# A sixth raw weight tile, in room taken from a work tile, the squares' buffer and the mixer's masks

## The chip, the cores and the metric

The kernel runs on one core of one Trainium2 chip. Its metric is the device time of one execution in microseconds (us). TensorE (PE) multiplies, VectorE (DVE) and ScalarE (ACT) prepare operands, GpSimd (POOL) and SyncE (SP) mostly issue transfers (DMAs).

## The reference

One layer of a decoder trunk, in float32: two feed-forward blocks around a mixer, with RMSNorm ahead of each and at the end.

```python
def rmsnorm(x, g):
    x32 = x.astype(jnp.float32)
    y = x32 * lax.rsqrt(jnp.mean(x32 * x32, axis=-1, keepdims=True) + EPS)
    return (y * g.astype(jnp.float32)).astype(x.dtype)

def swiglu(h, w_gate, w_up, w_down):
    return (jax.nn.silu(h @ w_gate) * (h @ w_up)) @ w_down
```
```text
x = x + 0.5 * SwiGLU_1(RMSNorm(x))
h = RMSNorm(x)
[attn_q|attn_k|attn_v|m_q|m_k|m_v|m_o|m_i|m_f] = h @ W_in
y_A = differential attention (4 heads, causal; weights a[0] - lam * a[1], lam from exps of two sums of lambda products)
y_B = mLSTM matrix memory (4 heads, causal conv on q/k, exp input gate, sigmoid forget gate, chunks of 128)
x = x + concat(y_A, y_B) @ W_out
x = x + 0.5 * SwiGLU_2(RMSNorm(x))
out = RMSNorm_final(x)
```

256 positions, model width 2048, feed-forward width 5632. All weights are float32 and each is read from memory once.

## The kernel before

**Products in two parts.** A float32 product is made of three single-pass products. Each weight tile `w` is split into `wh`, its rounding to the fast format (fp32r, a cast on ACT, line 132), and `wl = w - wh` (a subtraction on DVE, line 133); the activations are split the same way. PE then runs `wh*xh` (L181), `wh*xl` (L182) and `wl*xh` (L184). The parts lie in a pool of four pairs.

**Paired chunks.** Most weights go through the class `Paired`, which computes two output chunks of 512 columns (gate and up, or two neighbours) with fewer products than one by one, from sums of weight tiles. `load` (L446 and L208) fetches one raw tile, `raw`, with 256 KB of the one matrix and 512 KB of the other; a chunk has five such tiles (two or three in the down projections), fetched through POOL's queue, or SP's for the first chunks. `leading` multiplies the first slot and makes sums in place on DVE (L479); `second_sum` multiplies them and adds again, by an accumulating DMA on POOL (`raw<-raw`, L495) or on DVE (L497); `sums` adds a third weight tile `late` by accumulating DMA (`raw<-late`, L533), copies two finished banks with ACT into the work tiles `ds` and `us` (L503), and subtracts them on DVE (L537, L546). `second` and `third` follow, with unpaired weight tiles `rawp` (L219) between. A `raw` tile is free when its last split is done. Such a tile comes from the pool `wr`, of five buffers.

**Pools and order.** Tiles come from pools of fixed numbers of buffers; asking for a tile when all are in use makes the first instruction on it wait for the release of the oldest. Work tiles (pool `work`, tag `w`, eight buffers of 2 KB a partition) hold `xg`, `xsum`, `hg`, `sg`, `ds`, `us`, `part` and the mixer's small tiles, the lambda vectors `lv` among them; larger tiles come from 22 `slots`. A list scheduler fixes each engine's order when the program is built, from priorities (`tc.high_priority`, `soon`) and the buffers that are free in its own account of time. On the chip each engine runs its list strictly in order and waits on semaphores.

**Finishing a chunk of the residual.** `residual` (for the first block) and `finish2` (for the last) add half of an accumulator to `xres` on DVE (L359, L1211), then take the sum of squares of that piece for the next norm with `square_sum` (L300, ACT, with a separate instruction that reads the accumulator). The squares themselves are thrown away, into a buffer `junk`, one in all, of its own pool tag. `finish2` also multiplies by the final norm's gains (`fn`, L1213). `chunk_to_xt` transposes `xres` on PE (L314) for the next product.

**The start of the mixer.** `lv` is loaded by one POOL DMA (L768), two rows of it are multiplied on DVE (L769), reduced to `lsum` (L771), and ACT takes `lexp = exp(lsum)` (L773), which needs a table load. Masks for the causal products (`mask_qk`, `mask_kq`), a bf16 identity, a matrix of ones and an upper triangle are made on POOL at the very start of the program (L106 to L122) and kept; the mixer's small columns lie in pools `const` and `small`.

## Time and profile before

| | us |
|---|---|
| median of 3 runs | 1759.2 |
| lowest and highest | 1758.26, 1760.3 |
| profiled execution, its own time | 1759.56 |
| its span (first to last instruction) | 1757.8 |
| PE busy in the span | 1744.6 |
| DVE busy | 1617.8 |
| ACT busy | 1267.4 |
| POOL busy | 429.3 |

The clock granted to TensorE was 0.999. Times within the trace count from the start of the span. In the timeline views a row is: start, duration, engine, line, operation, tile written and tiles read, shape, how many in a row, and in brackets the engine's idle time just before with what ended it. In the groups it is busy time and mean, then idle time and its releasers. L181 is line 181 of the kernel before; the changed kernel's lines are 12 to 16 lower up to the mixer.

### The profile page before, as it was taken

What the parts mean: (1) busy time and instruction counts of PE and PEld (TensorE: products, weight loads), DVE (VectorE), ACT (ScalarE), POOL (GpSimd) and SP (SyncE); (2) the same over time, 40 slices, a digit from 0 to 9 for tenths busy, and PEclk for the clock granted to TensorE, in tenths of its full rate; (3) what the DMA queues carried; (4) which work ended last, traced back from release to release, by engine and by line L of the source; (5) the groups of instructions that cost most, each with busy time, mean ns of one, the idle gap of its engine ahead of it and who ended that gap; (6) DMA issues with size and microseconds to landing.
All of it is one profiled execution on the core that took longest, in us unless ns stands there. A gap on an engine that the chain in (4) does not pass through costs nothing.

```text
span 1757.8 us, 24486 instructions
## 1 busy us (share of the span) xinstructions
PE 1744.6 (99%) x7926; PEld 1437.7 (82%) x7926; DVE 1617.8 (92%) x2189; ACT 1267.4 (72%) x1949; POOL 429.3 (24%) x630
## 2 busy tenths in 40 slices
PE   9999999999999999999999999999999999999998
PEld 7788888888888888987888888888888878888886
DVE  7999999999999999898888999999999999999997
ACT  8666777777677768777687777776777677677765
POOL 0022332322233312012231101122332332233310
PEclk9999999999999999999999999999999999999999
DMA  9787998999799977577886667898998999799973
GB/s 365 251 254 209 259 261 265 253 292 265 218 262 258 263 252 204 185 230 221 236 238 192 209 210 211 260 265 233 258 260 268 241 268 276 232 246 256 283 254 115
DMA packets 155265, 429.72 MB, mean 244 GB/s; under 512 B 17632, under 2 KB 18944, under 8 KB 154880
## 3 DMA queue, kind: packets, MB, share of 16 engines
q0 software_dynamic: 76304, 196.66, 45.1%
q1 hardware_dynamic: 77680, 229.40, 38.0%
q10 hardware_dynamic: 1152, 2.09, 0.3%
q8 instruction: 62, 1.02, 0.2%
q14 instruction: 67, 0.55, 0.1%
HBM read 349.56 MB, written 2.10 MB: 200 GB/s over the span
## 4 chain that ended last, share of the span: by engine, by line
PE 93%; DMA 2%; DVE 2%; issue 1%; ACT 0%; POOL 0%; SPq 0%; POOLq 0%; DVEq 0%; ACTq 0%
PE acc L184 18%; PE acc L181 18%; PE acc L182 18%; PE accn L181 12%; PE accn L182 12%; PE accn L184 12%; DVE wl L133 1%; DMA raw<-in_wg_dram 1%; PE tr L373 1%; DMA raw<-in_wu_dram 1%; PE tr L314 0%; PE sc L1060 0%; DMA rawp<-in_wg_dram 0%; ACT wh L132 0%; PE num L1011 0%
## 5 line engine op out<-in xcount | busy, mean ns | idle before, releaser
L132 ACT CAST wh<-raw 128x512 fp32r<-128x512 f32 (+2 forms) x885 | 601.5, 708 | 214.5 <-PE acc L182 66.3
L133 DVE TENSOR_TENSOR wl<-raw,wh 128x512 fp32r<-128x512 f32 (+2 forms) x885 | 676.1, 793 | 58.4 <-ACT wh L132 54.5
L132 ACT CAST wh<-rawp 128x1024 fp32r<-128x1024 f32 (+3 forms) x308 | 318.2, 1035 | 109.5 <-PE acc L182 55.1
L133 DVE TENSOR_TENSOR wl<-rawp,wh 128x1024 fp32r<-128x1024 f32 (+3 forms) x308 | 367.1, 1197 | 32.0 <-ACT wh L132 29.8
L181 PE MATMUL acc<-wh,xs 128*128 128x512 f32 (+2 forms) x956 | 369.5, 387 | 0.0
L182 PE MATMUL acc<-wh,xs 128*128 128x512 f32 (+2 forms) x956 | 368.9, 386 | 0.0
L184 PE MATMUL acc<-wl,xs 128*128 128x512 f32 (+2 forms) x956 | 317.6, 387 | 0.8 <-DVE wl L133 0.7
L533 POOL DMA_DIRECT2D raw<-late x176 | 152.6, 1053 | 442.7 <-DVE wl L133 422.9
L181 PE MATMUL acc<-wh,xt 128*128 128x512 f32 (+2 forms) x564 | 218.4, 388 | 0.7 <-ACT wh L132 0.7
L182 PE MATMUL acc<-wh,xt 128*128 128x512 f32 (+2 forms) x564 | 217.3, 386 | 0.0
L181 PE MATMUL accn<-wh,xt 128*128 128x512 f32 (+1 forms) x552 | 215.3, 391 | 0.0
L182 PE MATMUL accn<-wh,xt 128*128 128x512 f32 (+1 forms) x552 | 214.7, 390 | 0.0
L479 DVE TENSOR_TENSOR raw<-raw 128x1024 f32<-128x1024 f32 x176 | 211.0, 1217 | 0.8
L184 PEld LDWEIGHTS acc<-wl,xs 128*128 128x128 f32 x956 | 178.3, 188 | 39.2 <-DVE wl L133 3.6
L181 PEld LDWEIGHTS acc<-wh,xs 128*128 128x128 f32 x956 | 179.5, 188 | 36.4 <-ACT wh L132 0.6
L182 PEld LDWEIGHTS acc<-wh,xs 128*128 128x128 f32 x956 | 179.6, 188 | 35.6
L181 PE MATMUL accn<-wh,xs 128*128 128x512 f32 (+1 forms) x408 | 162.6, 400 | 1.9 <-ACT wh L132 1.9
L182 PE MATMUL accn<-wh,xs 128*128 128x512 f32 (+1 forms) x408 | 158.0, 388 | 0.0
L184 PE MATMUL acc<-wl,xt 128*128 128x512 f32 (+2 forms) x564 | 157.6, 386 | 0.0
L495 POOL DMA_DIRECT2D raw<-raw x92 | 78.9, 899 | 322.1 <-DVE wl L133 234.7
L184 PE MATMUL accn<-wl,xt 128*128 128x512 f32 (+1 forms) x552 | 154.7, 388 | 0.0
L184 PE MATMUL accn<-wl,xs 128*128 128x512 f32 (+1 forms) x408 | 140.9, 388 | 0.0
(229 smaller groups left out, 2125.0 us busy)
## 6 DMA issues: line engine op xcount, KB each, us to landing
rawp<-in_wd_dram SPq DMA_DIRECT2D x88, 512.0 KB, 5.6
raw<-late POOLq DMA_DIRECT2D x174, 256.0 KB, 5.3
raw<-in_wu_dram POOLq DMA_DIRECT2D x80, 512.0 KB, 8.4
rawp<-in_wu_dram SPq DMA_DIRECT2D x73, 512.0 KB, 5.1
rawp<-in_wg_dram SPq DMA_DIRECT2D x69, 512.0 KB, 5.2
raw<-raw POOLq DMA_DIRECT2D x92, 256.0 KB, 4.1
raw<-in_wd_dram POOLq DMA_DIRECT2D x44, 512.0 KB, 8.6
late<-in_wg_dram SPq DMA_DIRECT2D x41, 512.0 KB, 9.2
```

The source lines that it names most:

```text
L132: return (nc.scalar.copy(hi, src), nc.vector.tensor_tensor(out=lo, in0=src, in1=hi.bitcast(F32), op=ALU.subtract))
L133: nc.vector.tensor_tensor(out=lo, in0=src, in1=hi.bitcast(F32), op=ALU.subtract))
L181: nc.tensor.matmul(acc, lh, rh, start=first, stop=False, skip_group_check=on)
L182: nc.tensor.matmul(acc, ll, rh, start=False, stop=False, skip_group_check=on)
L184: newest[:] = [nc.tensor.matmul(acc, lh, rl, start=False, stop=last, skip_group_check=on)]
L373: nc.tensor.transpose(tr[:, i, hb * P:(hb + 1) * P], hs[hb][:, k * P:(k + 1) * P], ident)
L479: nc.vector.tensor_tensor(out=raw[:, 0:2, :], in0=raw[:, 0:3:2, :], in1=raw[:, 1:2, :].to_broadcast([P, 2, n]), op=ALU.add)
L495: nc.gpsimd.dma_start(raw[:, 0, :], raw[:, 2, :], accum_op=ALU.add)
L533: nc.gpsimd.dma_start(self.raws[j][:, 0, :], lates[-1][1][:, i, :], accum_op=ALU.add)
```

## The change

`wr` grows from five raw tiles to six, `work` shrinks from eight to seven. `square_sum` writes its squares into a work tile, so that they no longer have a buffer of their own. The masks, the ones, the triangle and the bf16 identity are made at the start of the mixer, on POOL, in one large tile `masks` from the slots (the identity's copy on POOL rather than on DVE), and the mixer's small columns (`lsum`, `lexp`, `nlam`, `gatt`, `gp`, the attention's maxima and sums and so on) are cut from the same tile by `ct`.

```diff
--- before.py
+++ after.py
@@ -64,8 +64,8 @@
     const = ctx.enter_context(tc.tile_pool(name="const", bufs=1))
     big = ctx.enter_context(tc.tile_pool(name="big", bufs=1))
     slots = ctx.enter_context(tc.tile_pool(name="slots", bufs=22))
-    work = ctx.enter_context(tc.tile_pool(name="work", bufs=8))
-    wr = ctx.enter_context(tc.tile_pool(name="wr", bufs=5))
+    work = ctx.enter_context(tc.tile_pool(name="work", bufs=7))
+    wr = ctx.enter_context(tc.tile_pool(name="wr", bufs=6))
     wrp = ctx.enter_context(tc.tile_pool(name="wrp", bufs=5))
     wsp = ctx.enter_context(tc.tile_pool(name="wsp", bufs=4))
     small = ctx.enter_context(tc.tile_pool(name="small", bufs=2))
@@ -103,23 +103,8 @@
     nc.gpsimd.memset(ident, 0.0)
     nc.gpsimd.affine_select(out=ident, in_=ident, compare_op=ALU.not_equal, fill=1.0, base=0,
                             pattern=[[-1, P]], channel_multiplier=1)
-    ones = const.tile([P, P], F32, name="ones")
-    nc.gpsimd.memset(ones, 1.0)
-    upper = const.tile([P, P], F32, name="upper")
-    nc.gpsimd.affine_select(out=upper, in_=ones, compare_op=ALU.is_ge, fill=0.0, base=0,
-                            pattern=[[1, P]], channel_multiplier=-1)
     mhalf = const.tile([P, 8], F32, name="mhalf")
     nc.gpsimd.memset(mhalf, -0.5)
-    ident_b = const.tile([P, P], BF16, name="ident_b")
-    nc.vector.tensor_copy(ident_b, ident)
-    mask_qk = const.tile([P, P], BF16, name="mask_qk")
-    nc.gpsimd.memset(mask_qk, 0.0)
-    nc.gpsimd.affine_select(out=mask_qk, in_=mask_qk, compare_op=ALU.is_ge, fill=NEG, base=0,
-                            pattern=[[-1, P]], channel_multiplier=1)
-    mask_kq = const.tile([P, P], BF16, name="mask_kq")
-    nc.gpsimd.memset(mask_kq, 0.0)
-    nc.gpsimd.affine_select(out=mask_kq, in_=mask_kq, compare_op=ALU.is_ge, fill=NEG, base=0,
-                            pattern=[[1, P]], channel_multiplier=-1)
     xres = big.tile([P, NT, D], F32, name="xres")
 
     def split_gain(src, gcol, hi, lo):
@@ -296,8 +281,7 @@
         return r
 
     def square_sum(src, acc, scale=1.0):
-        j = small.tile([P, CW], BF16, tag="junk", name=nm("junk"), bufs=1)
-        nc.scalar.activation(j[:, 0:src.shape[-1]], src, AF.Square, scale=scale, accum_out=acc)
+        nc.scalar.activation(wk("junk")[:, 0:src.shape[-1]], src, AF.Square, scale=scale, accum_out=acc)
 
     def finish_norm(parts):
         tot = small.tile([P, NT], F32, tag="tot", name=nm("tot"))
@@ -764,17 +748,37 @@
     bif = const.tile([P, 8], F32, name="bif")
     with tc.issue_after(splits[-30][0].ins):
         nc.scalar.dma_start(bif, bias_if.partition_broadcast(P))
+    masks = mixt([P, 8 * P], name="masks")
+    ones, upper = masks[:, 0:P], masks[:, P:2 * P]
+    nc.gpsimd.memset(ones, 1.0)
+    nc.gpsimd.affine_select(out=upper, in_=ones, compare_op=ALU.is_ge, fill=0.0, base=0,
+                            pattern=[[1, P]], channel_multiplier=-1)
+    ident_b, mask_qk, mask_kq = (masks[:, (4 + i) * P // 2:(5 + i) * P // 2].bitcast(BF16) for i in range(3))
+    nc.gpsimd.tensor_copy(ident_b, ident)
+    for mask, sign in ((mask_qk, -1), (mask_kq, 1)):
+        nc.gpsimd.memset(mask, 0.0)
+        nc.gpsimd.affine_select(out=mask, in_=mask, compare_op=ALU.is_ge, fill=NEG, base=0,
+                                pattern=[[sign, P]], channel_multiplier=-sign)
+
+    taken = [4 * P]
+
+    def ct(shape, name):
+        o = taken[0]
+        taken[0] += math.prod(shape[1:])
+        t = masks[0:shape[0], o:taken[0]]
+        return t.rearrange("p (a b) -> p a b", a=shape[1]) if len(shape) > 2 else t
+
     lv = mixt([P, 4, P], name="lv")
     nc.gpsimd.dma_start(lv, lamv.partition_broadcast(P))
     nc.vector.tensor_tensor(out=lv[:, 0:2, :], in0=lv[:, 0:2, :], in1=lv[:, 2:4, :], op=ALU.mult)
-    lsum = const.tile([P, 2], F32, name="lsum")
+    lsum = ct([P, 2], "lsum")
     nc.vector.tensor_reduce(out=lsum, in_=lv[:, 0:2, :], axis=AX.X, op=ALU.add)
-    lexp = const.tile([P, 2], F32, name="lexp")
+    lexp = ct([P, 2], "lexp")
     nc.scalar.activation(lexp, lsum, AF.Exp)
-    nlam = const.tile([P, 1], F32, name="nlam")
+    nlam = ct([P, 1], "nlam")
     nc.vector.tensor_tensor(out=nlam, in0=lexp[:, 1:2], in1=lexp[:, 0:1], op=ALU.subtract)
     nc.vector.tensor_scalar(nlam, nlam, -LAM_INIT, None, op0=ALU.add)
-    gatt = const.tile([P, 8], F32, name="gatt")
+    gatt = ct([P, 8], "gatt")
     nc.vector.tensor_scalar(gatt, prm[:, G_ATT:G_ATT + 8], 1.0 - LAM_INIT, None, op0=ALU.mult)
 
 
@@ -826,7 +830,7 @@
 
 
     mT = [mixt([P, NH, S], name="mT") for _ in range(2)]
-    gp = const.tile([P, NT, 8], F32, name="gp")
+    gp = ct([P, NT, 8], "gp")
     heads = [0, 3, 6, 8]
 
     def finish_qk(c, accs):
@@ -855,9 +859,6 @@
     chain.finish()
     accs = []
     chain.put(units(accs, xp2, wqk[2], KD), KD // UK, functools.partial(finish_qk, 2, accs))
-
-    def ct(shape, name):
-        return const.tile(shape, F32, name=name)
 
     with tc.high_priority(offset=AHEAD + 40):
         gt = ct([P, NT, 8], "gt")
@@ -1050,8 +1051,8 @@
 
     def attend(h):
         q, k, o = qT[h // 2], kT[h // 2], 2 * (h % 2)
-        mx = small.tile([P, 4], F32, tag="amx", name=nm("amx"))
-        sm = small.tile([P, 4], F32, tag="asm", name=nm("asm"))
+        mx = ct([P, 4], "amx")
+        sm = ct([P, 4], "asm")
         e = mixt([P, 2, 3 * P], name="aexp")
         for hb in range(NT):
             n = (hb + 1) * P
@@ -1071,7 +1072,7 @@
         w = mixt([P, 3 * P], name="aw")
         for hb in range(NT):
             n = (hb + 1) * P
-            nl = small.tile([P, 1], F32, tag="nl", name=nm("nl"))
+            nl = ct([P, 1], "nl")
             vec.tensor_tensor(out=nl, in0=sm[:, 2 * hb + 1:2 * hb + 2], in1=nlam, op=ALU.mult)
             sl = slice(hb * P, hb * P + n)
             vec.tensor_scalar(w[:, sl], e[:, 1, sl], nl, None, op0=ALU.mult)
@@ -1114,7 +1115,7 @@
         nc.tensor.matmul(ps[:, 0, :], wts[h][:, 0:P], vs[0], start=True, stop=True)
         nc.tensor.matmul(ps[:, 1, :], wts[h][:, P:S], vs[0], start=True, stop=False)
         nc.tensor.matmul(ps[:, 1, :], wts[h][:, S:S + P], vs[1], start=False, stop=True)
-        ss = small.tile([P, NT], F32, tag="ssa", name=nm("ssa"))
+        ss = ct([P, NT], "ssa")
         for hb in range(NT):
             square_sum(ps[:, hb, :], ss[:, hb:hb + 1])
         ra = rsq(ss, NT, float(VD), "ra")
@@ -1166,7 +1167,7 @@
         return r3[0]
 
     fn = []
-    parts4 = [small.tile([P, 4], F32, tag=f"parts4{hb}", name=f"parts4{hb}") for hb in range(NT)]
+    parts4 = [small.tile([P, 4], F32, tag=f"parts4{hb}", name=f"parts4{hb}", bufs=1) for hb in range(NT)]
 
     def store(hb, acc):
```

The arithmetic is unchanged. The scheduler orders the instructions anew, and the order moves at these places.

POOL's queue, a gate-and-up chunk of the second block near the end (L446 and L208 load a raw tile's two parts, L495 and L533 are the accumulating DMAs; L430, L193, L479 and L517 in the changed kernel). Before, from the last accumulate of one chunk on:

```order
L533 DMA raw_15270<-late_15369 128x512
L446 DMA raw_15577<-in_wg_dram 128x512
L208 DMA raw_15577<-in_wu_dram 128x1024
L446 DMA raw_15580<-in_wg_dram 128x512
L208 DMA raw_15580<-in_wu_dram 128x1024
L446 DMA raw_15615<-in_wg_dram 128x512
L208 DMA raw_15615<-in_wu_dram 128x1024
L446 DMA raw_15618<-in_wg_dram 128x512
L208 DMA raw_15618<-in_wu_dram 128x1024
L446 DMA raw_15667<-in_wg_dram 128x512
L208 DMA raw_15667<-in_wu_dram 128x1024
L495 DMA raw_15577<-raw_15577 128x512
```

Now, the same place:

```order
L517 DMA raw_15220<-late_15319 128x512
L430 DMA raw_15530<-in_wg_dram 128x512
L193 DMA raw_15530<-in_wu_dram 128x1024
L430 DMA raw_15565<-in_wg_dram 128x512
L193 DMA raw_15565<-in_wu_dram 128x1024
L430 DMA raw_15568<-in_wg_dram 128x512
L193 DMA raw_15568<-in_wu_dram 128x1024
L430 DMA raw_15617<-in_wg_dram 128x512
L193 DMA raw_15617<-in_wu_dram 128x1024
L430 DMA raw_15933<-in_wd_dram 128x512
L193 DMA raw_15933<-in_wd_dram 128x1024
L479 DMA raw_15527<-raw_15527 128x512
```

The chunk's first pair (`raw_15527`) went out ahead of the accumulates of the chunk before, and the first pair of the following one (`in_wd`) stands at the end of this group. The other paired chunks have moved alike.

DVE's queue at the start of the mixer (L133 and L118 are the splits, L359 and L343 the residual update, `lv` the lambda vectors). Before:

```order
L133 TENSOR_TENSOR wl_6608<-late_6588,wh_6607 128x784
L133 TENSOR_TENSOR wl_6618<-raw_6482,wh_6617 128x392
L133 TENSOR_TENSOR wl_6618<-raw_6486,wh_6617 128x392
L359 SCALAR_TENSOR_TENSOR xres<-acc_6120,xres 128x512
L133 TENSOR_TENSOR xs_6514<-xg_6511,xs_6514 128x512
L133 TENSOR_TENSOR wl_6635<-rawp_6632,wh_6634 128x784
L537 TENSOR_TENSOR acc_6481<-acc_6481,us_6604 128x392
L133 TENSOR_TENSOR wl_6681<-raw_6482,wh_6680 128x784
L133 TENSOR_TENSOR xs_6386<-xsum_6382,xs_6386 128x512
L546 TENSOR_TENSOR acc_6480<-ds_6586,acc_6480 128x392
L769 TENSOR_TENSOR lv_6429<-lv_6429 128x256
```

Now:

```order
L782 TENSOR_SCALAR masks_6413<-prm 128x8
L118 TENSOR_TENSOR xs_6353<-xsum_6349,xs_6353 128x512
L118 TENSOR_TENSOR xs_6370<-xsum_6366,xs_6370 128x512
L773 TENSOR_TENSOR lv_6425<-lv_6425 128x256
L343 SCALAR_TENSOR_TENSOR xres<-acc_6104,xres 128x512
L775 TENSOR_REDUCE masks_6413<-lv_6425 128x2
L118 TENSOR_TENSOR wl_6599<-late_6579,wh_6598 128x784
L118 TENSOR_TENSOR xs_6505<-xg_6502,xs_6505 128x512
L118 TENSOR_TENSOR wl_6609<-raw_6473,wh_6608 128x392
L118 TENSOR_TENSOR wl_6609<-raw_6477,wh_6608 128x392
```

The multiply of `lv`, one residual update and the reduce to `lsum` (now a column of `masks`) have moved ahead of the split of `late` and those of the raw pair; the multiply stood ten rows behind that split before. On ACT the table load and the exponential have moved with them, ahead of two squares, `ds`, `us` and the cast of the next `rawp`.

ACT's queue near the end of the second block (L132 and L117 are the casts, L300 and L284 the squares, L503 and L487 the copies `ds` and `us`). Before:

```order
L503 COPY ds_16377<-acc_16277 128x512
L132 CAST wh_16408<-late_16379 128x1024
L300 ACTIVATE junk_16255,parts_10132<-xres 128x512
L132 CAST wh_16418<-late_16395 128x512
L132 CAST wh_16425<-raw_16278 128x512
L132 CAST wh_16425<-raw_16281 128x512
L503 COPY us_16405<-acc_16276 128x512
```

Now:

```order
L117 CAST wh_16358<-late_16329 128x1024
L284 ACTIVATE junk_16205,parts_10082<-xres 128x512
L284 ACTIVATE junk_16320,parts_10081<-xres 128x512
L284 ACTIVATE junk_16324,parts_10082<-xres 128x512
L487 COPY ds_16327<-acc_16227 128x512
L487 COPY us_16355<-acc_16226 128x512
L117 CAST wh_16368<-late_16345 128x512
L117 CAST wh_16375<-raw_16228 128x512
L117 CAST wh_16375<-raw_16231 128x512
```

Two more squares, `ds` and `us` now precede the second cast of `late`. The same pattern, smaller, stands at the ends of the first block and of the output projection.

## Prediction

> **What bounds the kernel now.** I read the page's first part, then the busy time by stretches, then PE's waits, and last the timelines of the places where the order of instructions changes. The profiled execution took 1759.56 us, its span 1757.8; 1.8 us lie around the span, and I keep them. It stands 0.4 us above the median of the runs shown, 1759.2.
>
> ```profile
> PE 1744.6 (99%) x7926; PEld 1437.7 (82%) x7926; DVE 1617.8 (92%) x2189; ACT 1267.4 (72%) x1949; POOL 429.3 (24%) x630
> ...
> 0.00:20.00 20.00, 16.80 (x63) 11.24 (x64) 13.40 (x28) 15.11 (x26) 1.92 (x13) 1.00 0.86 325
> ...
> 690.00:710.00 20.00, 20.00 (x110) 18.71 (x109) 19.30 (x38) 17.34 (x32) 5.23 (x8) 1.00 0.78 216
> ...
> 1300.00:1500.00 200.00, 199.41 (x888) 162.66 (x887) 188.80 (x242) 143.03 (x210) 58.89 (x87) 1.00 0.90 261
> ...
> 1700.00:1757.80 57.80, 49.24 (x222) 40.45 (x219) 47.41 (x72) 33.85 (x58) 4.01 (x5) 0.96 0.49 158
> ```
>
> Columns of the stretches: length, then PE, PEld, DVE, ACT, POOL busy, clock, DMA share, GB/s. PE is the bound: 13.2 us idle in the whole span, 3.2 of them in the first 20 us and 8.6 behind the last product. So more room for loads can win only what PE loses between, and every us that PE is held up costs a us. DVE, at 92%, is the engine with least room beside it, and between 690 and 710 it is busy 19.3 of 20 us: an idle us of DVE there is not made good.
>
> PE's idle time understates its stalls, because a product's modelled 0.39 us overlaps the next one, which starts 0.23 us later when nothing is late. The two largest:
>
> ```profile
> 1416.14 0.39 PE L184 MATMUL acc<-wl,xs 128*128 128x512 f32 x1
> 1417.06 0.50 PE L184 MATMUL acc<-wl,xs 128*128 128x512 f32 x1 [0.54 <-DVE wl L133]
> ...
> 1602.22 0.39 PE L184 MATMUL acc<-wl,xs 128*128 128x512 f32 x1
> 1602.77 0.50 PE L184 MATMUL acc<-wl,xs 128*128 128x512 f32 x1 [0.17 <-DVE wl L133]
> ```
>
> These lose 0.92 - 0.23 = 0.69 and 0.55 - 0.23 = 0.32 us. Counting every start in the two feed-forward stages (100 to 665 and 1040 to 1730 us) that comes over 0.1 us later than that pitch, 21 in all, I get 3.4 us. The mixer has next to none. How the stall at 1602 arises, on POOL and ACT:
>
> ```profile
> 1573.90 0.86 POOL L533 DMA_DIRECT2D raw<-late  x1 [2.09 <-DVE wl L133]
> 1581.52 0.57 POOL L446 DMA_DIRECT2D raw<-in_wg_dram  x1 [6.76 <-DVE wl L133]
> ...
> 1589.40 0.53 POOL L208 DMA_DIRECT2D raw<-in_wu_dram  x1 [0.15 <-issue]
> ...
> 1597.89 0.62 ACT L132 CAST wh<-raw 128x512 fp32r<-128x512 f32 x1 [3.62 <-DMA raw<-in_wg_dram]
> ```
>
> All five raw tiles are in use to the end of a chunk, so its successor's five load pairs leave in one burst, 1581.5 to 1589.9, behind the releases; the third takes 10.3 us to land and ACT idles 3.62 us for it.
>
> **The change, term by term.** (1) The sixth raw tile. On POOL each chunk's first load pair now stands ahead of the accumulates of the chunk before, into a tile that was freed long ago; each later pair takes the release that its predecessor took, and the burst shrinks from five pairs to four. A pair takes 1.1 us to issue (0.57 + 0.53), the accumulates behind it are delayed by that, and they wait for DVE far longer. At most this wins 3.4 us. The stalls at 1416 and 1602 hang on a late raw tile, smaller ones partly on DVE's own load; I take three quarters, -2.6, bounds -1.3 (about the two largest with their followers) and -3.4.
>
> (2) The masks.
>
> ```profile
> 0.95 0.20 POOL L107 MEMSET ones<- 128x128 f32 x1
> ...
> 1.45 0.29 POOL L109 TENSOR_SCALAR_AFFINE_SELECT upper<-ones 128x128 f32<-128x128 f32 x1
> ```
>
> Six such POOL instructions and one DVE copy leave the start, where PE waits for data and they lie beside it: 0. Rebuilt near 694 us on POOL, three fills at 0.20, three selects at 0.29 and the copy, which no row shows on POOL (0.29 if like a select, 0.73 if like POOL's `rstd` of two columns), come to 1.8 to 2.2 us. They stand behind the lambda load, where POOL idled 6.16 us (row below), and are first read by the gates' sums many products later: 0. Without that cover the next raw load would leave 2 us later, the size of the stalls above.
>
> (3) The squares. They take a work tile in turn rather than the one `junk` buffer, and carry, as ACT's waits in the order show, only the wait for DVE's `xres`. Each square costs the same. But the scheduler now puts squares, residual updates and the copies `ds` and `us` in other places of DVE's and ACT's queues. I walk these queues with the durations of the trace. Largest is the start of the mixer:
>
> ```profile
> 693.34 1.23 POOL L768 DMA_DIRECT2D lv<-in_lamv_dram  x1
> 700.74 0.56 POOL L446 DMA_DIRECT2D raw<-in_win_dram  x1 [6.16 <-DVE wl L133]
> ```
> ```profile
> DMA to landing us min/median/max: 4.3/4.3/4.3
> ```
> ```profile
> 694.80 0.97 DVE L133 TENSOR_TENSOR wl<-late,wh 128x784 fp32r<-128x784 f32 x1
> ...
> 701.17 0.42 DVE L769 TENSOR_TENSOR lv<-lv 128x256 f32<-128x256 f32 x1
> ...
> 704.17 0.42 DVE L771 TENSOR_REDUCE lsum<-lv 128x2 f32<-128x256 f32 x1
> ```
> ```profile
> 696.89 0.87 ACT L132 CAST wh<-rawp 128x784 fp32r<-128x784 f32 x1
> 697.66 0.49 ACT L503 COPY us<-acc 128x392 f32<-128x392 f32 x1
> ...
> 698.80 0.63 ACT L300 ACTIVATE junk<-xres 128x512 bf16<-128x512 f32 x1
> 699.33 0.19 ACT L300 ACTIVATION_READ_ACCUMULATOR junk<-xres 128x1 f32 x1
> ...
> 704.55 1.28 ACT L773 ACT_TABLE_LOAD   x1
> 705.85 0.21 ACT L773 ACTIVATE lexp<-lsum 128x2 f32<-128x2 f32 x1
> ```
> ```profile
> 698.19 0.51 PE L184 MATMUL accn<-wl,xs 128*128 128x392 f32 x2
> 698.54 0.34 PE L181 MATMUL acc<-wh,xs 128*128 128x392 f32 x1
> ...
> 701.89 1.03 PE L314 MATMUL tr<-ident,xres 128*128 128x128 f32 x8
> ...
> 703.66 0.34 PE L184 MATMUL acc<-wl,xs 128*128 128x392 f32 x1
> ```
>
> `lv` (the lambda vectors) lands at 693.34 + 4.3 = 697.6. DVE multiplied it at 701.17, when it was long there; now the multiply stands ahead of `wl<-late`. Ahead of it come two `xs` differences, the last `xsum` steps and the gain column, so DVE gets to it at 695.5 and idles 2.1 us. Multiply, one `xres` update (0.6) and the reduce: `lsum` at 699.0; `wl<-late`, needed by PE at 698.6 (698.19 and four of the eight transposes, 1.03 / 2 less their overlap, which now stand ahead of it), comes at 699.9: PE loses 1.3. What is queued behind the multiply on DVE is all of the next weight splits, and PE waits for those. On ACT the table load and the exponential now stand ahead of two squares, `ds`, `us` and the cast of `rawp`: exponential done at 699.5, squares 701.0, `ds` 701.4, `us` 701.9, cast 702.7. PE's next product, due 700.7, overwrites the bank that `us` copies, and starts at 701.9; then `wl<-rawp` is ready at 704.0. Where the trace of before ends the following group at 703.84, I get 706.5: **+2.7**. Bounds: +1.5 if `lv` lands by 696.4, +5.3 if it takes the 6.9 us that a 256 KB load takes (row below).
>
> ```profile
> raw<-in_wg_dram POOLq DMA_DIRECT2D x80, 256.0 KB, 6.9
> ```
>
> The Trainium skill puts a table switch at about 1.28 us of load and 1.38 us of drain (ScalarE: Activation LUTs, "What ACT_TABLE_LOAD costs"). This trace agrees on the load (1.28) and shows the exponential 0.02 us behind it, with no drain. With that drain ACT's chain from the exponential on would come up to 1.4 us later and the time at about 1762.8; since the row shows none, that has a chance of 0.02, out of the slower rival's.
>
> (4) The same kind near the end of the second feed-forward stage:
>
> ```profile
> 1720.01 0.58 ACT L503 COPY ds<-acc 128x512 f32<-128x512 f32 x1
> ...
> 1721.77 0.63 ACT L300 ACTIVATE junk<-xres 128x512 bf16<-128x512 f32 x1 [0.23 <-DVE xres L1211]
> ...
> 1722.40 0.61 ACT L132 CAST wh<-late 128x512 fp32r<-128x512 f32 x1
> 1723.67 1.14 ACT L132 CAST wh<-raw 128x512 fp32r<-128x512 f32 x2 [0.66 <-ACT wh L132]
> 1724.76 0.59 ACT L503 COPY us<-acc 128x512 f32<-128x512 f32 x1
> ```
> ```profile
> 1725.92 0.39 PE L181 MATMUL accn<-wh,xs 128*128 128x512 f32 x1
> ...
> 1727.96 0.39 PE L181 MATMUL acc<-wh,xs 128*128 128x512 f32 x1
> ```
>
> Two more squares (0.63 and the 0.19 read, 0.73 as they overlap), `ds` and `us` now stand ahead of `wh<-late`, and the squares wait for two more DVE updates of 0.6. ACT: squares done 1723.7, 1724.4, 1725.1, `ds` 1725.6, `us` 1726.1, `wh<-late` 1726.7 (due 1725.92), `wh<-raw` 1727.75; DVE's `wl<-raw` 1728.65. PE reaches at 1729.1 what it reached at 1727.96: **+1.2**, bounds +0.5 and +1.9.
>
> (5) At the end of the first stage two squares, `ds` and `us` come ahead of `wh<-late` at 666: it is ready at 669.6 for a use at 669.4, and the raw pair at 670.65 for one at 669.86: +0.7 (0 to 1). The same pattern at the end of the mixer's output projection has leads of 1.2 to 1.9 us, which cover it: +0.2 (0 to 0.5).
>
> Sum: -2.6 + 2.7 + 1.2 + 0.7 + 0.2 = +2.2 us, 1761.8 for the profiled execution, **1761.4** against the median. That is 0.13%; about 0.2%, 3.5 us, is what a measurement of this kernel can tell from no change.
>
> **Rivals.** *Slower:* the lambda load decides. It is one small DMA in a queue that carries weights; in before it had 3.5 us to spare (697.6 to 701.2), now DVE and ACT both stop for it, and each us of lateness is a us of PE. From 1.3 us of extra lateness (landing 699) the whole is over 0.2%; with the 6.9 us of a weight load, +2.6: 1764.0. For it: DVE at 92% leaves little to catch up with. Against: 4.3 us is measured, at an unchanged place behind the same two accumulates. Chance 0.29, with the other walked places at their upper ends.
>
> *Faster:* the leads before these places cover the moved work, and the burst's end wins all 3.4 us, perhaps 0.5 more at the start, where the third raw pair leaves earlier: 1755.3. For it: earlier weight tiles give ACT more freedom everywhere. Against: at 690 to 710 the moved work waits for a DMA, and the queues are in order; a raw tile that is there sooner does not help DVE past `lv`. Chance 0.12.
>
> *It does nothing:* the 366 us that loads wait for releases (row below) are nearly all hidden behind other tiles, one pair less in the burst moves the rest by too little, and what is held up in the walked places is made good by slack: 1759. Chance 0.10.
>
> ```profile
> POOL raw L446 <- DVE wl L133: 366.3, 124, 8.2
> ```
>
> *Seven work tiles are too few:* were a square, `sg` or `ds` to wait for a tile and hold ACT and then PE by 0.1 us in some 40 places, that is +4: 1765.4. ACT's order in the steady chunks is unchanged and ACT is 72% busy. Chance 0.04.
>
> My forecast, both signs of term at about their sizes, has 0.45.
>
> **The numbers.** Slower than 1762.7 has the slower rival but for its mild end (0.26) and the work tiles (0.04); faster than 1755.7 the faster rival (0.12); within is the rest, 0.58. Range: low end with all 3.4 us won and half of the walked +4.8, 1758.2, and 1.2 below it towards the faster rival: 1757.0. High end: -1.3 + 3.9 (2.7 and 1.2 of lateness) + 1.9 + 1.0 + 0.5 = +6.0, 1765.2, and a little less since not all come together: 1764.8.
>
> **What would show it.** In the changed profile: ACT's waits of `wh` for DMA `raw<-in_wg_dram` fall well below 42.4 us and the stalls at 1416 and 1602 go (term 1); DVE idles about 2 us before `lv<-lv`, whose releaser is its DMA, near 695, and PE shows its largest stall of the middle within 10 us of it (term 3); PE stalls about 1.2 us near 1727 (term 4). I am wrong if `lv` is there when DVE asks for it, if stalls of PE vanish that no row here shows as late, or if ACT's squares wait for a tile.

## The result, and the profile after

The changed kernel takes **1802.85 us** (median of 4 runs, 1802.5 to 1804.41) against 1759.75 for the kernel before (4 runs beside it, 1758.26 to 1761.51): a ratio of 1.0244 [1.0231, 1.0256], 43 us slower. The prediction had 1761.4 and a range up to 1764.8. The direction to which it gave 0.30 came, and seven times as far as its farthest rival (+6.2 us) had it.

The page of the changed kernel, first part and the costliest PE groups; the instruction counts are the same as before but for one fewer on DVE and one more on POOL:

```profile
span 1801.2 us, 24446 instructions
...
PE 1785.0 (99%) x7926; PEld 1441.0 (80%) x7926; DVE 1624.7 (90%) x2188; ACT 1272.6 (71%) x1949; POOL 434.0 (24%) x631
```

The span is 43.4 us longer, and PE's busy time 40.4 us longer, 1785.0 for 1744.6, with as many instructions. DVE and ACT grow by 7 and 5 us. So PE is not kept waiting; its own work got longer. Its waits, in the view that sums them by what ended them, stay small, and most of those that term 1 was about are gone from ACT's (PE's waits after, then ACT's row before and after):

```profile
PE accn L166 <- ACT wh L117: 1.7, 3, 0.7
PE accn L166 <- ACT accn L487: 1.7, 1, 1.7
PE accn L169 <- DVE wl L118: 1.5, 2, 1.3
PE accn L99 <- DVE touch L88: 1.3, 1, 1.3
PE acc L166 <- ACT us L487: 0.9, 1, 0.9
```
```profile
ACT wh L132 <- DMA raw<-in_wg_dram: 42.4, 31, 3.6
```
```profile
ACT wh L117 <- DMA raw<-in_wg_dram: 4.3, 5, 1.3
```

(Us in total, times, longest.) The groups by line and shape tell where the time lies. Before, one product of three kinds and a weight load (busy time, mean ns of one):

```profile
L181 PE MATMUL acc<-wh,xs 128*128 128x512 f32 x914 | 356.8, 390 | 0.0
L182 PE MATMUL acc<-wh,xs 128*128 128x512 f32 x914 | 356.2, 390 | 0.0
...
L182 PEld LDWEIGHTS acc<-wh,xs 128*128 128x128 f32 x956 | 179.6, 188 | 35.6
```

and the same after:

```profile
L166 PE MATMUL acc<-wh,xs 128*128 128x512 f32 x914 | 362.8, 397 | 0.0
L167 PE MATMUL acc<-wh,xs 128*128 128x512 f32 x914 | 362.1, 396 | 0.0
...
L167 PEld LDWEIGHTS acc<-wh,xs 128*128 128x128 f32 x956 | 179.9, 188 | 40.9
```

Same operation, shape, operands and count, and each 6 to 7 ns longer, while the weight load keeps its 188 ns. The timeline of PE at 300 us shows it product by product; before:

```profile
300.16 0.39 PE L181 MATMUL acc<-wh,xs 128*128 128x512 f32 x1
...
301.52 0.39 PE L181 MATMUL acc<-wh,xt 128*128 128x512 f32 x1
```

Six products lie between these two starts (two of L181, two of L182, two of L184): 1.36 / 6 = 0.227 us. After:

```profile
299.81 0.40 PE L169 MATMUL accn<-wl,xs 128*128 128x512 f32 x1
300.05 0.40 PE L169 MATMUL acc<-wl,xs 128*128 128x512 f32 x1
300.28 0.40 PE L166 MATMUL accn<-wh,xs 128*128 128x512 f32 x1
...
301.91 0.40 PE L167 MATMUL accn<-wh,xt 128*128 128x512 f32 x1
```

Nine products: 2.10 / 9 = 0.233 us, with no wait shown. It is so in every stage (233.2 to 233.3 ns in each of the six that I take apart, between 20 and 1720 us). In the busy time by stretches, 300 to 500 us (length, PE busy with its instructions, clock, DMA share, GB/s), first of before, then of after:

```profile
300.00:500.00 200.00, 200.00 (x893) 1.00 0.90 257
```
```profile
300.00:500.00 200.00, 200.00 (x870) 1.00 0.89 249
```

PE is busy for all 200 us in both, at a granted clock of 1.00 in both, and gets 23 products less done. Taken from start to start over all products of 512 columns (7045 and 7055 of the 7158; behind the rest there is a stall or an instruction of another kind), the mean is 227.3 ns before and 233.3 ns after: 5.94 ns more. 7158 x 5.94 ns = 42.5 us, of the 43.4 us by which the span grew. Products of 384 columns kept their pitch (173.7 and 173.6 ns), so did those of 392 (179.0 and 178.4). In long undisturbed runs of products the two pitches are 226.7 and 233.3 ns; the expectations below use these.

What can change a product's own pace, with the order, the operands and the clock the same? Buffers moved. In the built programs, in bytes within a partition:

| | `slots` (the activations' parts, stationary) | `wh` (weights' parts, moving) | `wh` less `slots`, modulo 256 |
|---|---|---|---|
| before | from 36640 | from 194592 | 0 |
| after | from 33888 | from 195904 | 224 |

The masks and columns that left `const` moved everything behind them down by 2752 bytes, both operands alike. What changed the distance lies between the two pools: a raw tile more (6144 bytes) and a work tile less, together 4064 bytes, so that a work tile takes 2080. That is 32 short of 4096. The full tiles of both pools are 4096 bytes and the operands of 512-column products begin at multiples of 512 bytes in them, so one number holds for all of these products.

### The profile page after: what moved, and what is told of

The parts are those of the page before. It is cut to its first block, busy times and chain, and to the rows that moved or that the text cites. A ratio compares the mean times of both kernels' runs of the same rounds, so it can differ in the third digit from the quotient of the medians.

```text
span 1801.2 us, 24446 instructions
## 1 busy us (share of the span) xinstructions
PE 1785.0 (99%) x7926; PEld 1441.0 (80%) x7926; DVE 1624.7 (90%) x2188; ACT 1272.6 (71%) x1949; POOL 434.0 (24%) x631
## 4 chain that ended last, share of the span: by engine, by line
PE 97%; DMA 1%; ACT 1%; DVE 1%; issue 1%; SPq 0%; POOLq 0%; POOL 0%; ACTq 0%; DVEq 0%
PE acc L166 19%; PE acc L167 19%; PE acc L169 19%; PE accn L166 12%; PE accn L169 12%; PE accn L167 12%; PE tr L357 1%; DMA raw<-late 0%; PE sc L1061 0%; PE tr L298 0%; DMA rawp<-in_wg_dram 0%; DVE wl L118 0%; PE num L1012 0%; PE tr L1100 0%; ACT wh L117 0%
## 5 line engine op out<-in xcount | busy, mean ns | idle before, releaser
L117 ACT CAST wh<-raw 128x512 fp32r<-128x512 f32 (+2 forms) x885 | 598.3, 706 | 204.8 <-PE acc L167 93.2
L118 DVE TENSOR_TENSOR wl<-raw,wh 128x512 fp32r<-128x512 f32 (+2 forms) x885 | 675.7, 792 | 65.1 <-ACT wh L117 47.6
L117 ACT CAST wh<-rawp 128x1024 fp32r<-128x1024 f32 (+3 forms) x308 | 317.5, 1033 | 129.3 <-PE acc L167 66.5
L118 DVE TENSOR_TENSOR wl<-rawp,wh 128x1024 fp32r<-128x1024 f32 (+3 forms) x308 | 366.9, 1196 | 40.5 <-ACT wh L117 37.6
L166 PE MATMUL acc<-wh,xs 128*128 128x512 f32 (+2 forms) x956 | 375.5, 393 | 0.9 <-ACT us L487 0.9
L167 PE MATMUL acc<-wh,xs 128*128 128x512 f32 (+2 forms) x956 | 374.7, 393 | 0.0
L169 PE MATMUL acc<-wl,xs 128*128 128x512 f32 (+2 forms) x956 | 322.9, 393 | 0.0
L517 POOL DMA_DIRECT2D raw<-late x176 | 155.0, 1069 | 480.7 <-DVE wl L118 451.0
L166 PE MATMUL acc<-wh,xt 128*128 128x512 f32 (+2 forms) x564 | 221.8, 394 | 0.7 <-ACT wh L117 0.7
L167 PE MATMUL acc<-wh,xt 128*128 128x512 f32 (+2 forms) x564 | 220.7, 392 | 0.0
L166 PE MATMUL accn<-wh,xt 128*128 128x512 f32 (+1 forms) x552 | 218.1, 395 | 0.0
L167 PE MATMUL accn<-wh,xt 128*128 128x512 f32 (+1 forms) x552 | 217.9, 395 | 0.0
L166 PE MATMUL accn<-wh,xs 128*128 128x512 f32 (+1 forms) x408 | 164.9, 405 | 3.5 <-ACT wh L117 1.7
L167 PE MATMUL accn<-wh,xs 128*128 128x512 f32 (+1 forms) x408 | 160.3, 394 | 0.0
L479 POOL DMA_DIRECT2D raw<-raw x92 | 80.7, 932 | 289.0 <-DVE wl L118 248.4
```

Of the source, the lines that this page charges most:

```text
L117: return (nc.scalar.copy(hi, src), nc.vector.tensor_tensor(out=lo, in0=src, in1=hi.bitcast(F32), op=ALU.subtract))
L118: nc.vector.tensor_tensor(out=lo, in0=src, in1=hi.bitcast(F32), op=ALU.subtract))
L166: nc.tensor.matmul(acc, lh, rh, start=first, stop=False, skip_group_check=on)
L167: nc.tensor.matmul(acc, ll, rh, start=False, stop=False, skip_group_check=on)
L169: newest[:] = [nc.tensor.matmul(acc, lh, rl, start=False, stop=last, skip_group_check=on)]
L479: nc.gpsimd.dma_start(raw[:, 0, :], raw[:, 2, :], accum_op=ALU.add)
```

## The experiments

e1 to e5 have the instruction order of the kernel they derive from; only addresses differ. "The kernel before" was run beside them each time: 1760.89, 1760.63, 1761.76 and 1760.76 us by call. e2 to e6 and e9 to e12 have one run each.

### Is it the address, and which?

Three theories stood at the start: A, the moving tile's start counts by itself (before it lies 32 bytes past a multiple of 64, after on one); B, its distance from the stationary tile counts; C, addresses have nothing to do with it (the sixth tile, the squares' work tile, the mixer's tile).

**e1**: the changed kernel with 32 unused bytes ahead of the split weights.

```diff
+    pad0 = ctx.enter_context(tc.tile_pool(name="pad0", bufs=1))
+    pad0.tile([P, 8], F32, name="pad0")
     wsp = ctx.enter_context(tc.tile_pool(name="wsp", bufs=4))
```

> The changed kernel with 32 unused bytes a partition ahead of the pool of wh and wl, which move from 195904 (a multiple of 64) to 195936 (32 above one, as in the kernel before); the order of instructions on every engine is the changed kernel's. In the changed kernel's trace a product of 512 columns starts every 233.3 ns, before every 226.7; 7157 of them at 6.67 ns are 47.7 us. Theory A (where the moving operand starts modulo 64 bytes sets the pitch): 226.7 ns again, 1755 to 1764 us. Theory B (the phase of the moving operand against the stationary one, xs and xt, which start 32 above a multiple of 64): 226.7 ns too, the same time. Theory C (the pitch comes from something else that the change did, an added raw tile or other transfers at the same moments): 233.3 ns and 1803 us stay.

Measured: **1764.22 us** (10 runs), ratio to before 1.0019 [1.0009, 1.0028]. 32 bytes took away 38.6 of the 43 us, to just above the 1755 to 1764 that A and B gave. Its row, and its stretch:

```profile
L168 PE MATMUL acc<-wh,xs 128*128 128x512 f32 x914 | 357.6, 391 | 0.0
```
```profile
300.00:500.00 200.00, 200.00 (x891) 1.00 0.91 256
```

C falls: sixth tile, squares and masks are all still there. **e2**, the same 32 bytes in the kernel before, with room for them from `parts4` (as in the change):

```diff
+    pad = ctx.enter_context(tc.tile_pool(name="pad", bufs=1))
+    pad.tile([P, 8], F32, name="pad")
     wsp = ctx.enter_context(tc.tile_pool(name="wsp", bufs=4))
...
-    parts4 = [small.tile([P, 4], F32, tag=f"parts4{hb}", name=f"parts4{hb}") for hb in range(NT)]
+    parts4 = [small.tile([P, 4], F32, tag=f"parts4{hb}", name=f"parts4{hb}", bufs=1) for hb in range(NT)]
```

> The kernel before with the same 32 bytes ahead of wh and wl, which move from 194592 to 194624, a multiple of 64 (the room comes from two buffers that are never used); the order of instructions is that of before. Theories A and B: 233.3 ns a product and about 1759 + 45 = 1800 to 1807 us. Theory C: 226.7 ns and 1759 us.

Measured: 1798.69 us, a little under the 1800 to 1807 of A and B, and 38 us slower than the kernel before, by nothing but 32 bytes:

```profile
L184 PE MATMUL acc<-wh,xs 128*128 128x512 f32 x914 | 361.6, 396 | 0.0
```

**e3**: the changed kernel with the 32 bytes ahead of `slots`, so that stationary and moving tiles move together.

```diff
+    pad0 = ctx.enter_context(tc.tile_pool(name="pad0", bufs=1))
+    pad0.tile([P, 8], F32, name="pad0")
     slots = ctx.enter_context(tc.tile_pool(name="slots", bufs=22))
```

> The changed kernel with the 32 bytes ahead of the slots, so that all pools behind them move: the stationary operands to 33920, a multiple of 64, the moving ones to 195936, 32 above one. Theory A: 226.7 ns and 1755 to 1764 us. Theory B: the phases still differ by 32, so 233.3 ns and 1803 us. Theory C: 1803 us.

Measured: 1803.72 us, and 396 to 397 ns a product. The moving tiles lie exactly where e1 has them (195936), and it did not help. **e4** goes the other way: the small tile `mhalf` is moved from `const` behind the pools, so that `slots` start 32 bytes lower, and 32 bytes ahead of `wsp` put the moving tiles back to where the change has them.

```diff
-    mhalf = const.tile([P, 8], F32, name="mhalf")
+    mhalf = small.tile([P, 8], F32, name="mhalf", bufs=1)
```

> The changed kernel with the stationary operands at 33856 and the moving ones at 195904, both multiples of 64 (one 32-byte constant moved behind them, 32 unused bytes between). Theory A: 233.3 ns and 1803 us. Theory B: the phases agree, so 226.7 ns and 1755 to 1764 us. Theory C: 1803 us.

Measured: 1763.3 us; the mean product takes 390 to 391 ns, as before. The moving tiles are at 195904, the address of the slow kernel. A falls with e3 and e4, and B holds: the distance counts. **e5** asks whether it is the distance to the stationary tiles or that to the tiles that ACT, DVE and the DMAs use beside them: `slots` 32 bytes lower as in e4, with the 32 bytes put right behind them, so that every other pool stays where the change has it.

```diff
     slots = ctx.enter_context(tc.tile_pool(name="slots", bufs=22))
+    pad = ctx.enter_context(tc.tile_pool(name="pad", bufs=1))
+    pad.tile([P, 8], F32, name="pad")
...
-    mhalf = const.tile([P, 8], F32, name="mhalf")
+    mhalf = small.tile([P, 8], F32, name="mhalf", bufs=1)
```

> In the runs that decided for the phase, other pools moved with the slots. Here the changed kernel has its slots (the stationary xs and xt) at 33856, a multiple of 64, and every pool behind them (work, raw, rawp, wh and wl) where the changed kernel has it, wh at 195904. Theory B (phase of moving against stationary operand): equal phases, 226.7 ns a product and 1762 to 1766 us. Theory D (phase of wh and wl against the tiles that ACT, DVE and the transfers touch): unchanged against the changed kernel, 233.3 ns and 1803 us.

Measured: 1763.81 us, 390 to 391 ns. Against the changed kernel only the slots moved, with `xres` and the constants made after `mhalf`, which the 512-column products do not read; their two operands are what must fit.

### Which distances are good?

**e6** was to sweep 16 distances in one run: the kernel before, where each new pair of split tiles starts 4 bytes further on, in tiles 64 bytes longer, with one `rawp` tile less for the room. Its total says nothing.

```diff
+    shift = [0]
...
-        return (pool.tile(shape, F32R, tag=tag + "h", name=nm(tag + "h")),
-                pool.tile(shape, F32R, tag=tag + "l", name=nm(tag + "l")))
+        a, n = shape[1], shape[2]
+        shift[0] = (shift[0] + 1) % 16
+        return tuple(pool.tile([P, a * n + 16], F32R, tag=tag + s, name=nm(tag + s))[:, shift[0]:shift[0] + a * n]
+                     .rearrange("p (a b) -> p a b", a=a) for s in "hl")
```

> The kernel before with wh and wl tiles of 64 more bytes, in which each new pair starts 4 bytes further than the last, round 16 starts; four rawp tiles rather than five make the room, so its time as a whole says nothing. What counts is the time from one 512-column product to the next by the distance of the moving from the stationary start. Theory E (it goes by lines of 64 bytes): 226.7 ns only where the distance is a multiple of 64, 233.3 at the 15 others. Theory F (by halves of 64 bytes): 226.7 at distances that leave both starts in the same half, 233.3 in the other half. Since neighbouring tiles lie 4160 bytes apart, it also shows whether a distance of 64 modulo 128 is as good as one of 0.

Measured: 1803.68 us. The mean pitch by distance shows a pattern of 16 bytes (229.4, 230.5, 231.0 and 230.4 ns at 12, 28, 44 and 60 bytes modulo 64; 237.1, 235.5, 236.3 and 237.8 at 4, 20, 36 and 52), but no distance gives 226.7, not even the 76 products at 0 modulo 256 (231.5). It decided nothing between the expectations: when neighbouring products read tiles at different offsets, a product's own distance is not the whole story. I had changed two things, distance and its uniformity.

So one distance a kernel, in four kernels: before with four `rawp` tiles and 16, 32, 48 or 64 unused columns of 4 bytes. The four share one instruction order.

```diff
-    wrp = ctx.enter_context(tc.tile_pool(name="wrp", bufs=5))
+    wrp = ctx.enter_context(tc.tile_pool(name="wrp", bufs=4))
+    pad = ctx.enter_context(tc.tile_pool(name="pad", bufs=1))
+    pad.tile([P, 16], F32, name="pad")
```

> The kernel before, with four pair raw tiles in place of five and 64 unused bytes ahead of the split weights: the moving start then lies 2368 modulo 4096 above the stationary start, where the four kernels with a pitch of 226.7 ns have 2304 and the three with 233.3 ns 2272, 2272 and 2336. The total says nothing, since a raw tile is missing; the pitch of 512-column products does. If only the remainder modulo 64 counts (Theory E): 226.7 ns. If the two starts must agree modulo 128 or more (Theory F): about 233 ns.

> As the run before it, with 128 unused bytes: distance 2432 modulo 4096. If only the remainder modulo 64 or modulo 128 counts: pitch of 512-column products 226.7 ns. If the two starts must agree modulo 256 or more: about 233 ns. Should both runs show a pitch between the two values, the distance acts in more than two steps.

> Four pair raw tiles and 192 unused bytes ahead of the split weights; only the pitch of 512-column products counts. Shifts of 0, 64 and 128 bytes gave 226.7, 229.2 and 232.6 ns. If the pitch grows with the shift and repeats every 256 bytes (Theory G): above 232 ns here, since 224 gave 233.3. If it repeats every 512 bytes, no value follows. If it were symmetric about 128 bytes: 229.2 ns.

> As the run before it, with 256 unused bytes. If the pitch repeats every 256 bytes (Theory G): 226.7 ns. If the period is 512 bytes, the longest that the kernel before allows, since its products lie at 256 and at 768 modulo 1024 and show one pitch: another value, 233 ns if 0 modulo 512 is the bad case.

Totals 1776.99, 1799.42, 1804.19 and 1769.89 us. The rows, of e9, e10, e11 and e12 in this order:

```profile
L184 PE MATMUL acc<-wh,xs 128*128 128x512 f32 x914 | 357.8, 391 | 0.0
L186 PE MATMUL acc<-wl,xs 128*128 128x512 f32 x914 | 311.2, 393 | 0.1
```
```profile
L184 PE MATMUL acc<-wh,xs 128*128 128x512 f32 x914 | 361.1, 395 | 0.0
```
```profile
L184 PE MATMUL acc<-wh,xs 128*128 128x512 f32 x914 | 361.1, 395 | 0.0
```
```profile
L184 PE MATMUL acc<-wh,xs 128*128 128x512 f32 x914 | 356.3, 390 | 0.0
```

By start-to-start times, with all other kernels that have one distance:

| distance modulo 256 | kernels | mean pitch, ns |
|---|---|---|
| 0 | before, e1, e4, e5, e12 | 227.3, 227.3, 227.3, 227.4, 227.4 |
| 32 | e2 | 233.3 |
| 64 | e9 | 229.2 |
| 128 | e10 | 232.6 |
| 192 | e11 | 233.3 |
| 224 | after, e3 | 233.3, 233.3 |

256 bytes bring the full pace back, 64, 128 and 192 do not: the rule repeats every 256 bytes, as Theory G had it (before, e1, e4 and e5 lie at 256 modulo 512, e12 at 0). E (modulo 64) and a symmetric form fall. So does the other half of G, that the pitch grows with the shift: 32 bytes give 233.3 ns, 64 give 229.2. The distance acts in more than two steps, and by what rule within the 256 bytes was not found. e12, at the full pace, is 9 us slower than the kernel before, by one run each; a `rawp` tile less, and with it the order of some of SP's loads, is what else it differs in. Above e12 the totals grow by less than the pitch (e11: 34.3 us, where 7158 x 5.9 ns is 42); slower products would cover part of that tile's waits, but this was only argued.

What stays open: how PE's two reads disturb one another, why the products of 384 and 392 columns mind so little (384 columns: 173.4 to 173.7 ns at 0, 32, 64 and 224, but 176.1 and 176.9 at 128 and 192), and what the sweep's 16-byte pattern has to do with it.

### The terms of the prediction, at the old pace

e1 is the change at the pace on which the prediction was made, and its trace can be laid beside that of before, product by product. Two more kernels take parts of it away.

**e7**: e1 with five raw tiles in `wr`, all else as in the change.

```diff
-    wr = ctx.enter_context(tc.tile_pool(name="wr", bufs=6))
+    wr = ctx.enter_context(tc.tile_pool(name="wr", bufs=5))
```

> The changed kernel with matched phases (32 bytes ahead of wh and wl) and five raw tiles instead of six; the order of ACT is the same, POOL and SP load as in the kernel before. What the sixth tile wins by itself is the difference to the matched run of 1764.2 us. My prediction's term: 2.6 us, so 1766.8. Rival (loads are not what holds PE): 1764.2, no difference.

Measured: 1765.61 us (7 runs), ratio to before 1.0032 [1.0018, 1.0046], where e1 has 1.0019. The sixth tile is worth 0.13%, 2.3 us by the ratios, 1.4 us by the medians of two calls; the intervals overlap, so PE's gain is not clear of noise. ACT's waits answer clearly, e1 first, then e7:

```profile
ACT wh L119 <- DMA raw<-in_wg_dram: 6.6, 7, 1.7
ACT wh L119 <- DMA raw<-late: 4.4, 6, 1.1
```
```profile
ACT wh L119 <- DMA raw<-in_wg_dram: 38.5, 30, 2.6
ACT wh L119 <- DMA raw<-late: 0.4, 2, 0.2
```

32 us less waiting of ACT is worth some 2 us of the whole, if that. The second row is new, and has a price at the start (below).

**e8**: e1 with the lambda load, product, sums and exponential (ten lines, `lv` to `nlam`) moved behind the gates' arithmetic, 110 lines down.

```diff
-    lv = mixt([P, 4, P], name="lv")
...
-    nc.vector.tensor_scalar(nlam, nlam, -LAM_INIT, None, op0=ALU.add)
     gatt = ct([P, 8], "gatt")
...
+    lv = mixt([P, 4, P], name="lv")
...
+    nc.vector.tensor_scalar(nlam, nlam, -LAM_INIT, None, op0=ALU.add)
```

> The changed kernel with matched phases and the lambda block (load, multiply, reduce, exponential) written after the gates' arithmetic, so that neither DVE nor ACT meets it at the start of the mixer; the squares, ds and us stay ahead of the next cast. In the matched run PE falls back 4.26 us between 678 and 707, in two stalls (1.49 on DVE's split behind the multiply, 1.20 on the copy us) and then 3 us at half clock. My theory: the first stall goes, the second stays at about 1.3, the half clock goes: 1764.2 - 2.7 = 1761.5 us, as the kernel before. Rival (the block only moves the wait to where it now stands): 1764.

Measured: 1762.08 us (11 runs), ratio 1.0005 [0.9996, 1.0013]: no difference from the kernel before, and 0.14% better than e1, 2.5 us, though the two intervals overlap a little. This is the best form of the change that was found; none beat the kernel before.

Where the traces at the old pace stand behind that of before, at the start of the same product, in us (e4 and e5 are e1 at other addresses):

| time in before | 75 | 310 | 645 | 678 | 707 | 1015 | 1114 | 1349 | 1452 | 1621 | 1749 |
|---|---|---|---|---|---|---|---|---|---|---|---|
| e1 later by | 1.11 | 0.81 | 1.45 | 1.27 | 5.53 | 5.52 | 6.22 | 6.37 | 4.77 | 4.11 | 4.93 |
| e4 later by | 0.88 | 0.58 | 0.60 | 0.44 | 3.69 | 3.65 | 4.48 | 5.17 | 3.58 | 2.90 | 3.86 |
| e5 later by | 1.41 | 1.08 | 1.14 | 0.96 | 4.40 | 4.42 | 5.23 | 5.27 | 4.27 | 3.60 | 4.44 |
| e7 later by | 0.58 | 0.29 | 1.59 | 1.41 | 5.63 | 5.67 | 6.44 | 6.55 | 5.71 | 5.08 | 5.96 |
| e8 later by | 1.41 | 1.16 | 1.24 | 1.07 | 2.39 | 2.31 | 3.05 | 3.44 | 2.25 | 1.61 | 2.49 |

The jump of e1 from 678 to 707, +4.26 us, is the start of the mixer. DVE of e1, then ACT, then PE:

```profile
695.93 1.37 DVE L120 TENSOR_TENSOR xs<-xsum,xs 128x512 fp32r<-128x512 f32 x2
699.11 0.43 DVE L775 TENSOR_TENSOR lv<-lv 128x256 f32<-128x256 f32 x1 [1.80 <-DMA lv<-in_lamv_dram]
...
700.38 0.97 DVE L120 TENSOR_TENSOR wl<-late,wh 128x784 fp32r<-128x784 f32 x1
```
```profile
699.96 1.28 ACT L779 ACT_TABLE_LOAD   x1
701.25 0.20 ACT L779 ACTIVATE masks<-masks 128x2 f32<-128x2 f32 x1
...
702.96 0.49 ACT L489 COPY us<-acc 128x392 f32<-128x392 f32 x1
```
```profile
699.59 0.49 PE L300 MATMUL tr<-ident,xres 128*128 128x128 f32 x3
701.40 0.62 PE L171 MATMUL accn<-wl,xs 128*128 128x392 f32 x2 [1.33 <-DVE wl L120]
...
703.50 0.69 PE L168 MATMUL acc<-wh,xs 128*128 128x392 f32 x1 [1.03 <-ACT us L489]
703.99 0.53 PE L169 MATMUL acc<-wh,xs 128*128 128x392 f32 x1
704.31 0.53 PE L168 MATMUL acc<-wh,xs 128*128 128x392 f32 x1
```

This is term 3 step by step: DVE waits 1.80 us for `lv`, `wl<-late` comes late and PE idles 1.33, the exponential, squares, `ds` and `us` stand in line on ACT, and PE idles 1.03 for `us`. In e8 only the second of these is left (1.01 us). But behind the second stall e1's products of 392 columns are 0.33 us apart, where they are 0.18 us apart at 697.69 to 698.41. The stretches of e1 around it, PE alone:

```profile
700.00:703.40 3.40, 1.14 (x7) 1.00 0.26 61
```
```profile
703.40:706.60 3.20, 3.10 (x9) 0.50 0.21 68
```
```profile
706.60:710.00 3.40, 3.40 (x20) 0.97 0.73 184
```

After 3.4 us in which PE was busy a third of the time, the granted clock fell to 0.50 for some 3.4 us: nine instructions in the 3.2 us shown, where the full clock does about twice as many. That is about 9 x 0.15 = 1.4 us behind the two stalls.

But it does not come each time. In e5, the same order of instructions, the same two stalls are there (1.69 and 0.67 us) and the clock stays up:

```profile
700.00:703.40 3.40, 1.28 (x7) 1.00 0.25 44
703.40:706.60 3.20, 2.82 (x15) 1.00 0.24 82
```

There, and in e4, PE falls back 3.44 and 3.25 us from 678 to 707; in e1, and in e7, where the clock fell too, 4.26 and 4.22. So the half clock was worth 0.8 to 1.0 us of e1's jump. The traces' records of the clock suggest why: e1's two changes here, at 703.39 and 706.80, are 3.41 us apart, and e4's first and last, at 4.20 and 1755.24, 513 times that. Counted on such a grid, PE was busy for 1.16 us in the one step of e1 that holds the stalls, while in e4 and e5 they fall into two steps, with at least 2 us each. That the grid decides was not tested.

## Why the prediction was wrong

**The step that failed** is not one of the five terms but the ground under all of them: term 3 walks the queues "with the durations of the trace" and says of the squares "each square costs the same", and so all five took it of the products, without a word. The prediction had a price for every instruction that the change adds or moves, and none for the addresses that it moves. The term that is missing is +42.5 us: 7158 products, each 5.94 ns slower, since the moving tiles lie 224 bytes modulo 256 from the stationary ones where they lay at 0. e1 and e2 show it both ways with 32 bytes. Nothing in the trace of before could price it, as all its products of 512 columns have one pitch; that one operand would move against the other was to be read from the diff (the two pools between them, `work` and `wr`, change size), and the prediction should have carried an unknown for it.

By that the rivals fall as well: neither the lambda load nor too few work tiles made the kernel slow, and "slower" came out for a reason that no rival named. In the changed kernel itself the other terms together are worth about 43.4 - 42.5 = +0.9 us, less than e1's: PE asks for its operands later, and more of the lateness may be covered, which no run takes apart.

Point by point at the old pace, by e1 (+4.8 us between the profiled executions, 1764.33 and 1759.56; +3.3 between the medians; predicted +2.2). That the sums lie near one another is in part luck, since the misses below have both signs:

- *Term 1, -2.6 (bounds -1.3 to -3.4).* Within its bounds by size, but not shown where it was said: e7 puts the tile at 1.4 to 2.3 us. The predicted sign in ACT's waits, well below 42.4, came: 4.3, and 6.6 in e1. The two quoted stalls went too; e1 wins 1.60 from 1349 to 1452 and 0.69 from 1586 (4.80) to 1621, where they were. But e7, with five tiles, wins 0.84 and 0.70 in the same places, and the two stalls are not in it, so the sixth tile is not what removed all of that; what did stays open. What e7 has more than the others is lateness before 645 (+1.30 from 310, where e4, e5 and e8 have at most +0.08 and e1 +0.64). A slip besides: the load that took 10.3 us to land, and for which ACT idled 3.62, is the fourth pair, issued at 1587.56, not the third.
- *Term 2, 0 with nothing at the start.* The masks' own price held: PE waits for none of them near 694. POOL took 2.8 us for them rather than 1.8 to 2.2, in a stretch in which it had nothing else to do. But the start lost time, which I had only as a gain. e1 is 1.11 us late at 75 us. Of that, 0.53 is there at 20 us already and is not the change's: in e1 the first products of 512 columns start 0.43 us apart until 10 us, in e8, the same program up to there, 0.23. The rest comes at 64 us, where ACT waits and before it did not:

```profile
63.87 1.05 ACT L119 CAST wh<-raw 128x1024 fp32r<-128x1024 f32 x1 [1.14 <-DMA raw<-late]
64.82 0.58 ACT L489 COPY accn<-acc 128x512 f32<-128x512 f32 x1
```
```profile
65.45 0.51 PE L168 MATMUL accn<-wh,xs 128*128 128x512 f32 x1 [0.55 <-ACT accn L489]
```

  The extra load pair went ahead of the accumulating load `raw<-late`, and the copy that PE needs is queued behind the cast that waits for it. The prediction had this very step ("the accumulates behind it are delayed by that, and they wait for DVE far longer"), but it did not hold here. The place costs 0.57 us in e1 and 0.8, 1.3 and 1.4 in e4, e5 and e8; e7, with five tiles, does not have this stall.
- *Term 3, +2.7 (bounds +1.5 to +5.3).* Mechanism right in every step, measured +4.26, and +3.25 and +3.44 in e4 and e5. The two stalls were sized at 1.3 and 1.2 us, and PE's idle rows have 1.33 and 1.03; what is missing most in e1 is the clock that falls behind them, 0.8 to 1.0 us, which e4 and e5 do not have. `lv` was 1.80 us late rather than 2.1. e8 shows that the lambda block caused it: without it the place costs +1.32.
- *The drain of a table load,* 1.38 us by the Trainium skill (ScalarE: Activation LUTs, "What ACT_TABLE_LOAD costs"), is not there in e1 either: table load at 699.96 for 1.28, exponential at 701.25, the next square at 701.36.
- *Term 4, +1.2 (bounds +0.5 to +1.9).* +0.8 (4.13 at 1720, 4.93 at 1749), with a PE wait of 0.34 for `wh` at 1730.55 of e1: the waits were foreseen, DVE's and ACT's leads a little larger than I walked them.
- *Term 5, +0.7 and +0.2.* The two places came out the other way round: -0.2 at the end of the first block (645 to 678), +0.70 between 1015 and 1114, where the output projection ends and the second block starts. Their sum, +0.5, lies near the +0.9 predicted.

So the walk through the queues was good to about 1.5 us in each place, and useless for the result.

## What to carry to other kernels

A change of pools moves buffers, and a matmul kernel that PE bounds can lose or gain some per cent by nothing else: before pricing such a change, compare the start addresses of moving and stationary operands in both builds, and keep their distance a multiple of 256 bytes (here, for fp32r products of 512 columns, a pad of 32 bytes a partition was worth 2.2%). If a result is far from every walked queue, first compare the mean time of the commonest instruction, by form, in both profiles; that row decides between "works slower" and "waits more" at once. A blocking load put ahead of queued work costs more than its own wait: all that is queued behind it on each engine comes late, and the granted clock may fall as well, as it did in two of the four traces at the old pace that have these stalls (0.8 to 1.0 us).

## What the runs showed of the hardware that I had not expected

- The pitch of a 512-column product with its own weight load, single-pass fp32r, was 227.3 ns with the two operands' starts at 0 modulo 256 bytes, 229.2 at 64, 232.6 at 128 and 233.3 at 32, 192 and 224. The Trainium skill gives PE two read ports, one for the moving operand and one for weight loads, independent of one another (SBUF — State Buffer, "Who interferes with whom"). In these runs the two reads are not without effect on one another: e5 changes only the place of the one operand relative to the other, and the pace with it. Whether they meet at a port or in the memory behind it, no run shows.
- The granted clock fell to 0.50 for 3.4 us in e1, after 3.4 us in which PE was busy for 1.14; in e5, where it was busy for 1.28 of 3.4, it did not. The Trainium skill has the half clock follow an idle window of about 3.4 us (TensorE: Matmul & The Clock Gate, "What's actually happening"). The length agrees with e1; there PE was not idle for the whole of it, but did a transpose or a product in between. How much work in a window keeps the clock up, these runs do not show.
